# A hybrid attention block: compressed scores moved to the front, another bank for the fourth transpose, an identity made on chip, a last tile in two halves

## The chip, the cores and the metric

The kernel runs on one core of a Trainium2 chip. The metric is the device time of one execution in microseconds; the median of three runs before the change is 832.62 us (832.56 to 832.69). The core has five engines that run their own instruction streams in order and wait for each other by semaphores: PE (TensorE, matmuls and transposes), DVE (VectorE), ACT (ScalarE), POOL (GpSimd) and SP (SyncE, which here issues loads and stores). PE writes only to PSUM, which has eight banks of 512 float32 values in each of 128 partitions; all other engines' operands of this kernel lie in SBUF or in these banks.

## The reference

One decoder layer on x of 512 tokens and 1024 columns. Cut to what matters:

```python
h = rmsnorm(x, attn_norm_g)
q, k_c, v_c, k_s, v_s, k_w, v_w, nsa_gate, rwkv_in, gate_a, gate_b = split(h @ w_in)
o_a = nsa_mixer(...)        # 8 query heads of 64 in 2 groups, three branches:
   # compressed: softmax(q . kc + bias_c) vc, kc/vc = a small MLP over blocks of 32 tokens, stride 16
   # selected:   softmax over chosen blocks of 64 tokens (16 chosen, of only 8 that there are)
   # window:     softmax over the last 512 tokens
   # o = gate0 * o_cmp + gate1 * o_slc + gate2 * o_win
o_b = rwkv7_mixer(...)      # a recurrence over the tokens, 8 heads of 64
merged = sigmoid(gate_a) * (o_a @ w_proj_a) + sigmoid(gate_b) * (o_b @ w_proj_b)
x = x + merged @ w_out
u = rmsnorm(x, ffn_norm_g) @ w_up          # 1024 -> 2 * 2816
c = causal depthwise conv of width 3 over u
x = x + (silu(c_gate) * c_value) @ w_down  # 2816 -> 1024
```

Everything is float32 in and out.

## The kernel before

**Products in halves.** Large products run as three matmuls in a rounded float32 type: each operand is split into a high part (`hh`, `whi`) and a low part (`hl`, `wlo`), and hi·hi, lo·hi and hi·lo are summed in one PSUM bank. Every matmul goes through the helper `mm` (L122), every activation through `act` (L125), the additions and products of two tiles through `tt` (L128) and those by a scalar through `ts` (L132), so many rows of the profile carry these lines. Weights come through a chain of three `raw` buffers: `wload` (SP's queue) loads, ACT makes `whi`, DVE or POOL makes `wlo` (L299).

**PSUM.** Eight banks in three rotating pools: `mmb()` four, `pa()` two, `pb()` two. A pool hands its banks out in turn; the new user waits until the last reader of the old content is done. In the attention the four of `mmb()` are fixed: `Ob` collects the outputs, `db[0]` and `db[1]` alternate under dense products, `tb3` helps with transposes.

**The start.** The four token tiles of x (128 tokens each) are loaded on SP's queue, then the first weights. ACT's queue loads the 128x128 identity (`ident`, the first columns of the tile `kc`, 64 KB) and a small vector; POOL issues eight small loads of the RWKV parameters into `pra`. ACT squares each tile, DVE makes its norm and scales it, PE transposes it with `ident` (L341); PE also transposes `pra` (L356). The tile `warm`, all ones, feeds 30 matmuls that only keep PE running while x arrives.

**The attention.** There are twelve units: for the last two query tiles (qt = 3, 2) one per group g and branch b, for the first two tiles one per group with both branches in it. A unit goes through `scores`, `scale`, `turns`, `values`:

- `scores(u, n, mid)`: for each chunk, one `pa()` bank, matmuls of the queries with the keys' high and low part (KH, KL); DVE adds the bias and finds the row's extreme in one custom operation (L1171), which is the bank's only reader; ACT takes the exponential into P. After each chunk come its share of `n` fillers and the next function of the list `mid`.
- `scale(u)`: DVE and ACT multiply P by the gate over the row's sum (L1184 and after).
- `turns(u)`: PE transposes P in tiles, four 128x128 to a bank (L1204); ACT or DVE copy each bank to a slot of PTs (L1110 to L1116).
- `values(u)`: PE multiplies the transposed P with the values into `Ob`, together with the compressed branch's part (sC with `vcb`).

`compressed(qt)` makes the compressed branch for a query tile: eight 64-wide matmuls (KC) into one `pa()` bank, two reads of that bank by DVE into sC, the softmax over 32 blocks on DVE and ACT, each row scaled by its gate. It is a generator that stops once, for qt = 3, after the second read. `compressed_t(qt)` transposes sC (L1149) and ACT copies it back.

**Fillers.** The products for the gates and for `w_proj_b` are cut into single matmuls; `filler(n)` issues n of them between the other work, so that PE has something to do while DVE and ACT work on a unit. Their two banks are `db`; `nd` counts the products begun, so `db[nd[0] % 2]` is the bank that the next one will take.

**What sets the order.** In the attention PE's order is written out by hand (`tc.manual_schedule(engines=KTS)`, KTS holds PE alone); the order on DVE, ACT and POOL comes from the scheduler of the framework. The handwritten order begins: scores and scale of unit 0, `compressed(3)` to its stop, scores of unit 1, turns of unit 0, the rest of `compressed(3)`, scores of unit 2 with `compressed_t(3)` after its first chunk, values of unit 0. At the start all of PE, ACT, DVE and POOL follow the order of the code.

**The end.** The down projection runs in two halves of 512 output columns (`dense_tok`, written as the generator `dense_tok_g`). Four banks collect four token tiles over 22 row tiles of `w_down`, two per weight load; the last two loads are walked token tile by token tile, so that a finished tile is added to x1 and stored while the next one runs. For the last tile of the second half the add is done in two pieces of 256 columns, the first stored through SP's queue, the second through ACT's.

Of the kernel before, what the change touches and what calls it, by code (L numbers as in the profile page):

```python
# [16 lines left out]
ALU = mybir.AluOpType  # L17
# [6 lines left out]
NT = S // 128  # L24
KT = D // 128
# [6 lines left out]
NF = DFF // 128  # L32
# [50 lines left out]
def hybrid_block(ctx: ExitStack, tc: tile.TileContext, A: dict, out: bass.AP):  # L83
    nc = tc.nc
    v, sc, te = nc.vector, nc.scalar, nc.tensor
# [32 lines left out]
    def pb():  # L118
        return bank("b", 2)

    def mm(o, l, r, start, stop):
        te.matmul(o, lhsT=l, rhs=r, start=start, stop=stop)  # L122
# [4 lines left out]
    def tt(o, a, b, op):  # L127
        v.tensor_tensor(o, a, b, op=op)  # L128
# [12 lines left out]
    ident, mask, ones, cmask = kc[:, 0:128], kc[:, 128:256], kc[:, 256:384], kc[:, 384:416]  # L141
# [9 lines left out]
    warm = xp.tile([128, 128], F32, name="warm")  # L151
# [2 lines left out]
    pr0 = xp.tile([8, 128], F32, name="pr0")  # L154
    for t in range(NT):
        nc.sync.dma_start(xt[:, t], x_in[128 * t:128 * t + 128])
    sc.dma_start(ident, A["consts"][:, 0:128])
    sc.dma_start(pr0, A["attn_norm_g"][0].rearrange("(r p) -> r p", p=128))
    pra = xp.tile([NR0, 128], F32, name="pra")
    for name in ("rwkv_mu", "rwkv_w0", "rwkv_a0", "rwkv_k_k", "rwkv_k_a", "rwkv_r_k", "rwkv_ln_g", "rwkv_ln_b"):  # L160
        r0, n = ROWS[name]
# [170 lines left out]
    with tc.manual_schedule(engines={getattr(mybir.EngineType, e) for e in ("PE", "Activation", "DVE", "Pool")}):  # L332
# [10 lines left out]
        for t in range(NT):  # L343
            r = ssx[:, t:t + 1]
# [8 lines left out]
            if t == 1:  # L353
                pt = pts[7][:, 384:512]
# [5 lines left out]
        r0, n = ROWS["rwkv_mu"]  # L360
# [26 lines left out]
    def run(g):  # L387
        while True:
            try:
                next(g)  # L390
            except StopIteration as e:
                return e.value
# [223 lines left out]
    for g in range(2):  # L616
        for b in range(2):
            r = 64 * g + 32 * b
            v.transpose(Nn[r:r + 32].rearrange("p t s -> p t s"),
                        ABq[g][r:r + 32, :, 32 * b:32 * b + 32].rearrange("p q t -> p t q"))  # L620
    for k in range(31):
        m, n = 31 - k, k + 1
# [4 lines left out]
        stt(Tn[:, k + 1:, 0:n], tmv, 1.0, Tn[:, k + 1:, 0:n], ALU.mult, ALU.add)  # L627


    def dense_tok_g(n, xh, xl, kt=KT, halves=False):  # L630
        banks = [mmb() for _ in range(NT)]
        step = 1024 // n
        tiles = [list(range(k0, min(k0 + step, kt))) for k0 in range(0, kt, step)]

        def passes(parts, ts_):
            for part in range(2):
                for ks, w in parts:
                    for i, k in enumerate(ks):
                        for t in ts_:
                            qs = slice(128 * t, 128 * t + 128)  # L640
                            if part == 0:
                                mm(banks[t][:, 0:n], xh[:, k, qs], w[0][:, i], k == 0, False)
                                mm(banks[t][:, 0:n], xl[:, k, qs], w[0][:, i], False, False)
                            else:
                                mm(banks[t][:, 0:n], xh[:, k, qs], w[1][:, i], False, k == kt - 1)
                    if len(ts_) > 1:
                        yield

        for j, ks in enumerate(tiles[:-2]):
            parts = [(ks, wnext(len(ks), n))]  # L650
            for ts_ in ([range(2), range(2, NT)] if halves and j == 0 else [range(NT)]):
                yield from passes(parts, ts_)
        last = [(ks, wnext(len(ks), n)) for ks in tiles[-2:]]
        for t in range(NT):
            yield from passes(last, [t])
            if t < NT - 1:
                yield
        return banks

    def dense_tok(*a, **kw):  # L660
        return run(dense_tok_g(*a, **kw))
# [5 lines left out]
    vt = m2.tile([128, NT, 2, 128], F32, name="vt")  # L667
# [28 lines left out]
    pt = pa()  # L696
# [35 lines left out]
    for b in (1, 0):  # L732
        for g in range(2):
            r = 64 * g + 32 * b
# [30 lines left out]
    fill = kv_proj(1, 280)  # L765
# [159 lines left out]
    fill = fill_chain()  # L925
# [142 lines left out]
    Ob, db, tb3 = mmb(), [mmb(), mmb()], mmb()  # L1068
    nd = [0]
# [26 lines left out]
    fill = fillers()  # L1096
# [3 lines left out]
            next(fill, None)  # L1100

    oaT = m2.tile([128, 2, NH2, S], F32R, name="oaT", tag="QK")
    ev, tn = [0], [0]
    Ps, PTk = {}, {}

    PTs = hp.tile([128, 8, S], F32, name="PTs", tag="hh")
# [45 lines left out]
    def scores(u, n, mid=()):  # L1152
        qt, g, bs = u
        qs = slice(128 * qt, 128 * qt + 128)
        N = 128 * (qt + 1)
        R = 4 * len(bs)
        P = Pb[units.index(u) % 4][:, 0:R * N].rearrange("p (r n) -> p r n", n=N)
        nm = at.tile([128, 8], F32, name="nm", tag="nm", bufs=2)
        sm = at.tile([128, 8], F32, name="sm", tag="sm", bufs=2)
        per = 4 // (qt + 1)  # L1160
        nb = R // per
        for i0 in range(0, R, per):
            sp = pa()
            for i in range(i0, i0 + per):
                h, b = 4 * g + i % 4, bs[i // 4]
                o = sp[:, N * (i - i0):N * (i - i0) + N]
                mm(o, qst[:, h, qs], KH[:, b, g, 0:N], True, False)
                mm(o, qst[:, h, qs], KL[:, b, g, 0:N], False, True)
            for i in range(i0, i0 + per):
                h = 4 * g + i % 4  # L1170
                v.tensor_tensor_reduce(out=P[:, i], in0=sp[:, N * (i - i0):N * (i - i0) + N], in1=BT[:, h, 384 - 128 * qt:512],  # L1171
                                       scale=-1.0, scalar=-NEG, op0=ALU.add, op1=ALU.min, accum_out=nm[:, i:i + 1])
                act(P[:, i], P[:, i], AF.Exp, scale=-1.0, bias=nm[:, i:i + 1], accum_out=sm[:, i:i + 1])
            ib = i0 // per
            filler(n * (ib + 1) // nb - n * ib // nb)
            if ib < len(mid):
                mid[ib]()
        Ps[u] = P, sm
# [16 lines left out]
    def turns(u):  # L1195
        qt, g, bs = u
        P, _ = Ps.pop(u)
        PTk[u] = []
        for x in range(len(bs)):
            for k in range(qt + 1):  # L1200
                pt = Ob if tn[0] == 3 else tb3 if (tn[0] - (tn[0] > 3)) % 3 == 2 else pb()
                tn[0] += 1
                for i in range(4):
                    te.transpose(pt[:, 128 * i:128 * i + 128], P[:, 4 * x + i, 128 * k:128 * k + 128], ident)  # L1204
                PTk[u].append((bs[x], k, evac(pt)))

    def values(u):
        qt, g, bs = u
        qs = slice(128 * qt, 128 * qt + 128)
        O = Ob[:, 256 * g:256 * g + 256]  # L1210
        if bs[0] == 0:
            sCT = sC2[:, qt % 2].rearrange("p h n -> p (h n)")
            for j in range(2):
                for e in range(2):
                    mm(O[64 * e:64 * e + 64, 128 * j:128 * j + 128], vcb[:, 2 * g + e], sCT[:, 128 * j:128 * j + 128],
                       j == 0, False)
        for b, k, PT in PTk.pop(u):
            for r in range(2):
                mm(O[64 * r:64 * r + 64].rearrange("p (a q) -> p a q", a=2), vt[:, k, b, 64 * g:64 * g + 64],
                   PT.rearrange("p (h q) -> p h q", h=4)[:, r::2, :], False, b == 1 and k == qt)  # L1220
        if bs[-1] == 1:
            ov = O.rearrange("p (a q) -> p a q", a=2)
            act(oaT[:, 0, 2 * g:2 * g + 2, qs], ov)
            tt(oaT[:, 1, 2 * g:2 * g + 2, qs], ov, oaT[:, 0, 2 * g:2 * g + 2, qs].bitcast(F32), ALU.subtract)

    units = [(qt, g, (b,)) for qt in (3, 2) for g in range(2) for b in range(2)]
    units += [(qt, g, (0, 1)) for qt in (1, 0) for g in range(2)]
    nfill = [5, 5, 6, 6, 7, 8, 10, 10, 10, 9, 9, 6]
    with tc.manual_schedule(engines=KTS):
        after_next = (1,2,3,4,5,6,7,8,9)  # L1230
        scores(units[0], 12)
        scale(units[0])
        comp = compressed(3)
        next(comp)
        scores(units[1], 12)
        for i, u in enumerate(units):
            turns(u)
            if i == 0:
                run(comp)
            if i in (4, 8, 10):  # L1240
                compressed_t(u[0])
            if i + 2 < len(units):
                mid = [lambda: None, functools.partial(scale, units[i + 1])] if i + 1 in after_next else [lambda: None, lambda: None]
                if i == 0:
                    mid.insert(0, functools.partial(compressed_t, 3))
                scores(units[i + 2], nfill[i], mid)
                if i + 2 not in after_next:
                    scale(units[i + 2])
            else:
                filler(nfill[i])  # L1250
            if i in (1, 5, 7):
                run(compressed({1: 2, 5: 1, 7: 0}[i]))
            values(u)
        filler(100)
# [63 lines left out]
    with tc.manual_schedule(engines=KTS):  # L1318
        for t in range(NT):
            qs = slice(128 * t, 128 * t + 128)  # L1320
            p = mmb()
# [50 lines left out]
        act(aT[:, 0, f], cv)  # L1372
        tt(aT[:, 1, f], cv, aT[:, 0, f].bitcast(F32), ALU.subtract)
    for hf in range(2):
        bo = dense_tok(512, aT[:, 0], aT[:, 1], NF)
        for t in range(NT):
            n = 256 if hf and t == NT - 1 else 512
            for c0 in range(0, 512, n):
                cs = slice(512 * hf + c0, 512 * hf + c0 + n)
                tt(x1[:, t, cs], x1[:, t, cs], bo[t][:, c0:c0 + n], ALU.add)  # L1380
                (sc if c0 else nc.sync).dma_start(out[0][128 * t:128 * t + 128, cs], x1[:, t, cs])
    close(fp_cm)
    close(xr_cm)
# [26 lines left out]
```

## Time and profile before

| what | value |
| --- | --- |
| median of three runs | 832.62 us |
| the profiled execution | 832.52 us |
| its span, first to last instruction | 830.7 us |
| granted TensorE clock | 1.000 |
| PE busy | 821.3 us, 99% of the span |
| DVE, ACT, POOL busy | 514.4, 406.2, 50.7 us |
| instructions | 12893, of them 5107 matmuls |
| moved by DMA | 78.73 MB |

The page gives busy time by engine, then the span in forty slices, then the DMA queues, then the chain of work that ended last, followed back from the last instruction. The list of waits gives, for one engine, the operation that waited and whom for, with total, number and longest. In the timeline a row is start, length, engine, line, operation, output and inputs with their shapes, how many instructions the row joins, and in brackets the idle time before the first of them and what ended it. PE's matmuls are pipelined: a record ends after the next has begun, so a step is the distance of two starts. PE's name for the weight load is PEld; an engine's name with q is its DMA issue.

### The profile page before, as it was taken

What the parts mean: (1) busy time and instruction counts of PE and PEld (TensorE: products, weight loads), DVE (VectorE), ACT (ScalarE), POOL (GpSimd) and SP (SyncE); (2) the same over time, 40 slices, a digit from 0 to 9 for tenths busy, and PEclk for the clock granted to TensorE, in tenths of its full rate; (3) what the DMA queues carried; (4) which work ended last, traced back from release to release, by engine and by line L of the source; (5) the groups of instructions that cost most, each with busy time, mean ns of one, the idle gap of its engine ahead of it and who ended that gap; (6) DMA issues with size and microseconds to landing.
All of it is one profiled execution on the core that took longest, in us unless ns stands there. A gap on an engine that the chain in (4) does not pass through costs nothing.

```text
span 830.7 us, 12893 instructions
## 1 busy us (share of the span) xinstructions
PE 821.3 (99%) x5107; PEld 669.1 (81%) x5107; DVE 514.4 (62%) x1008; ACT 406.2 (49%) x793; POOL 50.7 (6%) x67
## 2 busy tenths in 40 slices
PE   8999999999999999999999999999999999999998
PEld 7777778987777887787888988888888888888886
DVE  5577789975465878787765576656665556323222
ACT  6766655454455777785334554444444444221220
POOL 6100020140000210011000000000000000000000
PEclk9999999999999999999999999999999999999999
DMA  8432222246372410001274042333333333223421
GB/s 246 107 83 63 77 77 77 71 126 185 103 128 77 90 39 19 21 26 39 78 268 136 1 119 86 100 103 102 99 89 90 101 102 103 90 89 113 140 76 51
DMA packets 109400, 78.73 MB, mean 95 GB/s; under 512 B 3877, under 2 KB 98012, under 8 KB 109340
## 3 DMA queue, kind: packets, MB, share of 16 engines
q1 hardware_dynamic: 106800, 73.92, 31.1%
q10 hardware_dynamic: 1196, 2.55, 0.9%
q0 software_dynamic: 1344, 1.45, 0.8%
q8 instruction: 40, 0.66, 0.3%
q14 instruction: 20, 0.16, 0.1%
HBM read 74.56 MB, written 2.29 MB: 93 GB/s over the span
## 4 chain that ended last, share of the span: by engine, by line
PE 95%; DVE 3%; ACT 1%; DMA 0%; issue 0%; DVEq 0%; ACTq 0%
PE ps_mm L122 84%; PE ps_a L122 5%; PE ps_b L122 2%; PE ps_b L1204 1%; PE ps_mm L1204 1%; DMA xt<-in_x_dram 0%; DVE P L1171 0%; DVE sC L128 0%; ACT P L125 0%; DVE P L132 0%; PE ps_b L536 0%; PE ps_b L567 0%; DVE PTs L1116 0%; PE ps_a L1016 0%; PE ps_b L203 0%
## 5 line engine op out<-in xcount | busy, mean ns | idle before, releaser
L299 DVE TENSOR_TENSOR wlo<-raw,whi 128x1024 fp32r<-128x1024 f32 (+1 forms) x111 | 131.5, 1185 | 184.5 <-PE ps_mm L122 160.0
L122 PE MATMUL ps_mm<-hh,whi 128*128 128x512 f32 (+1 forms) x624 | 242.7, 391 | 0.5 <-DVE hl L137 0.5
L122 PE MATMUL ps_mm<-hl,whi 128*128 128x512 f32 (+1 forms) x624 | 240.5, 388 | 0.0
L125 ACT ACTIVATE whi<-raw 128x1024 fp32r<-128x1024 f32 (+3 forms) x124 | 123.3, 996 | 158.6 <-PE ps_mm L122 143.2
L122 PE MATMUL ps_mm<-hh,wlo 128*128 128x512 f32 (+1 forms) x624 | 152.1, 384 | 0.0
L122 PEld LDWEIGHTS ps_mm<-hh,whi 128*128 128x128 f32 x624 | 117.3, 188 | 27.2 <-issue 1.0
L122 PEld LDWEIGHTS ps_mm<-hl,whi 128*128 128x128 f32 x624 | 117.5, 188 | 22.9 <-issue 1.0
L122 PEld LDWEIGHTS ps_mm<-hh,wlo 128*128 128x128 f32 x624 | 115.2, 188 | 23.4
L122 PE MATMUL ps_mm<-whi,aT 128*128 128x512 f32 x352 | 84.5, 390 | 0.0
L122 PEld LDWEIGHTS ps_mm<-whi,aT 128*128 128x128 f32 x352 | 66.0, 188 | 14.3 <-issue 0.4
L137 DVE SCALAR_TENSOR_TENSOR cgv<-ps_mm,cw,cgv 128x511 f32<-128x511 f32 (+1 forms) x88 | 65.4, 746 | 1.6
L125 ACT ACTIVATE cgv<-ps_mm,cw 128x512 f32<-128x512 f32 x44 | 34.2, 780 | 23.3 <-PE ps_mm L122 23.3
L122 PE MATMUL ps_mm<-wlo,aT 128*128 128x512 f32 x176 | 44.3, 390 | 0.0
L125 ACT ACTIVATE aT<-cgv 128x512 fp32r<-128x512 f32 x22 | 13.9, 632 | 56.8 <-DVE cgv L128 56.8
L125 ACT ACTIVATE P<-P,nm 128x512 f32<-128x512 f32 (+3 forms) x64 | 35.4, 554 | 12.2 <-DVE nm L1171 12.0
L122 PEld LDWEIGHTS ps_mm<-wlo,aT 128*128 128x128 f32 x176 | 33.1, 188 | 6.9
L125 ACT ACTIVATE cgv<-cgv 128x512 f32<-128x512 f32 x22 | 13.9, 632 | 41.0 <-DVE cgv L137 41.0
L299 POOL TENSOR_TENSOR wlo<-raw,whi 128x512 fp32r<-128x512 f32 (+3 forms) x13 | 21.1, 1620 | 200.9 <-PE ps_mm L122 132.2
L1171 DVE CUSTOM_DVE_ANT_0 P<-ps_a,AB 128x512 f32<-128x512 f32 (+3 forms) x64 | 29.3, 486 | 4.1 <-PE ps_a L122 3.9
L128 DVE TENSOR_TENSOR x<-x,ps_mm 128x512 f32<-128x512 f32 (+1 forms) x17 | 11.0, 655 | 23.2 <-PE ps_mm L122 21.3
L128 DVE TENSOR_TENSOR aT<-cgv,aT 128x512 fp32r<-128x512 f32 x22 | 15.2, 693 | 14.7 <-ACT aT L125 14.7
L125 ACT ACTIVATE QK<-ps_mm 128x64 f32<-128x64 f32 (+5 forms) x56 | 14.8, 308 | 17.5 <-PE ps_mm L122 17.4
(357 smaller groups left out, 1206.0 us busy)
## 6 DMA issues: line engine op xcount, KB each, us to landing
raw<-in_w_up_dram SPq DMA_DIRECT2D x44, 512.0 KB, 3.8
raw<-in_w_in_dram SPq DMA_DIRECT2D x38, 512.0 KB, 3.9
raw<-in_w_down_dram SPq DMA_DIRECT2D x22, 512.0 KB, 3.6
raw<-in_w_out_dram SPq DMA_DIRECT2D x8, 512.0 KB, 4.0
xt<-in_x_dram SPq DMA_DIRECT2D x4, 512.0 KB, 4.1
raw<-in_cmp_w_v_dram SPq DMA_DIRECT2D x4, 512.0 KB, 3.8
raw<-in_w_proj_b_dram SPq DMA_DIRECT2D x8, 256.0 KB, 2.8
raw<-in_w_proj_a_dram SPq DMA_DIRECT2D x8, 256.0 KB, 2.7
```

Source lines behind the costliest of these rows:

```text
L122: te.matmul(o, lhsT=l, rhs=r, start=start, stop=stop)
L125: sc.activation(o, i, f, **kw)
L128: v.tensor_tensor(o, a, b, op=op)
L137: v.scalar_tensor_tensor(o, a, s, b, op0=op0, op1=op1)
L299: low = eng.tensor_tensor(lo, raw, hi.bitcast(F32), op=ALU.subtract)
L1171: v.tensor_tensor_reduce(out=P[:, i], in0=sp[:, N * (i - i0):N * (i - i0) + N], in1=BT[:, h, 384 - 128 * qt:512], scale=-1.0, scalar=-NEG, ...
L1204: te.transpose(pt[:, 128 * i:128 * i + 128], P[:, 4 * x + i, 128 * k:128 * k + 128], ident)
```

## The change

Five edits.

1. The identity is no longer loaded. POOL makes it by a selection on `warm` (ones where row and column number agree, zero elsewhere), placed behind the first of the eight `pra` loads in POOL's stream, where the instruction that configures POOL now stands too; the other seven loads follow it. ACT's queue loses one DMA.
2. The last token tile of the down projection's second half: the twelve 512-wide matmuls of its last two weight loads become 24 of 256. First all for columns 0 to 255 into the old bank, then all for columns 256 to 511 into a new bank of `pb()`. Columns 256 to 511 so end in two partial sums, and DVE adds both to x1, one 256-wide add more than before.
3. `compressed(3)` is run whole before the scores of unit 0; `compressed_t(3)` stands after the second score chunk of unit 2 in place of the first.
4. In `turns` the bank of a tile follows its place in the unit: two of `pb()`, then `tb3`, and a fourth tile takes `Ob` (unit 0) or the filler bank `db[nd[0] % 2]`. Before, one counter over all units rotated over `pb()`, `pb()`, `tb3`, with `Ob` once.
5. In `values` the products with PTs come first and open the accumulation; the compressed part comes last and closes it.

```diff
-    sc.dma_start(ident, A["consts"][:, 0:128])
+    nc.gpsimd.affine_select(ident, warm, pattern=[[-1, 128]], compare_op=ALU.is_equal, fill=0.0, base=0,
+                            channel_multiplier=1)
...
+        def split_end(parts):
+            qs = slice(128 * NT - 128, 128 * NT)
+            banks.append(pb())
+            for c0, o in ((0, banks[NT - 1][:, 0:256]), (256, banks[NT][:, 0:256])):
+                cs = slice(c0, c0 + 256)
+                for part in range(2):
+                    for ks, w in parts:
+                        for i, k in enumerate(ks):
+                            mm(o, xh[:, k, qs], w[part][:, i, cs], c0 > 0 and part == 0 and k == parts[0][0][0],
+                               part == 1 and k == kt - 1)
+                            if part == 0:
+                                mm(o, xl[:, k, qs], w[0][:, i, cs], False, False)
...
-            yield from passes(last, [t])
+            if ends and t == NT - 1:
+                split_end(last)
+            else:
+                yield from passes(last, [t])
...
-                pt = Ob if tn[0] == 3 else tb3 if (tn[0] - (tn[0] > 3)) % 3 == 2 else pb()
-                tn[0] += 1
+                j = len(PTk[u])
+                pt = pb() if j < 2 else tb3 if j == 2 else Ob if u == units[0] else db[nd[0] % 2]
...
+        PT = PTk.pop(u)
+        for b, k, T in PT:
+            for r in range(2):
+                mm(O[64 * r:64 * r + 64].rearrange("p (a q) -> p a q", a=2), vt[:, k, b, 64 * g:64 * g + 64],
+                   T.rearrange("p (h q) -> p h q", h=4)[:, r::2, :], b == 0 and k == 0, b == 1 and k == qt and len(bs) == 1)
         if bs[0] == 0:
...
-                       j == 0, False)
...
+                       False, j == 1 and len(bs) == 2)
...
+        run(compressed(3))
         scores(units[0], 12)
         scale(units[0])
-        comp = compressed(3)
-        next(comp)
         scores(units[1], 12)
         for i, u in enumerate(units):
             turns(u)
-            if i == 0:
-                run(comp)
...
-                    mid.insert(0, functools.partial(compressed_t, 3))
+                    mid.insert(1, functools.partial(compressed_t, 3))
...
-        bo = dense_tok(512, aT[:, 0], aT[:, 1], NF)
+        bo = dense_tok(512, aT[:, 0], aT[:, 1], NF, ends=hf == 1)
...
+                if c0:
+                    tt(x1[:, t, cs], x1[:, t, cs], bo[NT][:, 0:n], ALU.add)
```

More of the change, by code (lines that the diff above doesn't have):

```diff
@@ L627, in hybrid_block, with dense_tok_g @@
         stt(Tn[:, k + 1:, 0:n], tmv, 1.0, Tn[:, k + 1:, 0:n], ALU.mult, ALU.add)
-    def dense_tok_g(n, xh, xl, kt=KT, halves=False):
+    def dense_tok_g(n, xh, xl, kt=KT, halves=False, ends=False):
         banks = [mmb() for _ in range(NT)]
@@ L1102, in hybrid_block @@
     oaT = m2.tile([128, 2, NH2, S], F32R, name="oaT", tag="QK")
-    ev, tn = [0], [0]
+    ev = [0]
     Ps, PTk = {}, {}
@@ L1215, in values @@
                     mm(O[64 * e:64 * e + 64, 128 * j:128 * j + 128], vcb[:, 2 * g + e], sCT[:, 128 * j:128 * j + 128],
-                       j == 0, False)
[L1217 to L1220, printed above, removed]
+                       False, j == 1 and len(bs) == 2)
         if bs[-1] == 1:
```

## The prediction

> **What bounds the kernel now.** I read the page's busy shares first, then its chain, then the list of PE's waits, then the timeline where a wait is listed.
>
> ```profile
> span 830.7 us, 12893 instructions
> ...
> PE 821.3 (99%) x5107; PEld 669.1 (81%) x5107; DVE 514.4 (62%) x1008; ACT 406.2 (49%) x793; POOL 50.7 (6%) x67
> ...
> GB/s 246 107 83 63 77 77 77 71 126 185 103 128 77 90 39 19 21 26 39 78 268 136 1 119 86 100 103 102 99 89 90 101 102 103 90 89 113 140 76 51
> ...
> PE 95%; DVE 3%; ACT 1%; DMA 0%; issue 0%; DVEq 0%; ACTq 0%
> ```
> ```profile
> PE ps_mm L1204 <- ACT PTs L125: 0.6, 1, 0.6
> PE ps_mm L122 <- DVE hl L137: 0.5, 1, 0.5
> ```
>
> PE is busy in 99% of the span and makes 95% of the chain, and no edit takes a matmul away. All that can be won is idle time of PE: at the start, in the attention, and behind its last matmul. The waits listed are small because a record runs on past the start of the next one; stalls have to be read from start to start. First, what one step of PE costs:
>
> ```profile
> 823.96 1.98 PE L122 MATMUL ps_mm<-whi,aT 128*128 128x512 f32 x8
> 825.77 1.07 PE L122 MATMUL ps_mm<-wlo,aT 128*128 128x512 f32 x4
> ```
> ```profile
> 464.62 0.28 PE L122 MATMUL ps_mm<-hh,whi 128*128 128x256 f32 x1
> 464.74 0.28 PE L122 MATMUL ps_mm<-hl,whi 128*128 128x256 f32 x1
> ```
>
> Four more 512-wide matmuls take 1.98 − 1.07 = 0.91 us, 0.227 each (a last record is then 1.07 − 3 × 0.227 = 0.39 long). A 256-wide one steps by 0.12.
>
> **Compressed scores first.** PE's starts in the attention's first scores:
>
> ```profile
> 298.94 0.39 PE L122 MATMUL ps_a<-KH,qst 128*128 128x512 f32 x1
> ...
> 303.55 0.98 PE L122 MATMUL ps_a<-KC,qst 128*128 128x64 f32 x8
> ...
> 305.37 0.40 PE L122 MATMUL ps_mm<-hh,whi 128*128 128x512 f32 x1
> 305.87 0.50 PE L122 MATMUL ps_a<-KH,qst 128*128 128x512 f32 x1
> 306.20 0.39 PE L122 MATMUL ps_a<-KL,qst 128*128 128x512 f32 x1
> ...
> 306.66 0.62 PE L122 MATMUL ps_mm<-hh,wlo 128*128 128x512 f32 x2
> 307.48 0.47 PE L122 MATMUL ps_a<-KH,qst 128*128 128x512 f32 x1 [0.19 <-DVE sC L128]
> ...
> 312.09 0.40 PE L122 MATMUL ps_mm<-obT,whi 128*128 128x512 f32 x1
> 312.95 0.41 PE L1149 MATMUL ps_mm<-kc,sC 128*128 128x128 f32 x2 [0.46 <-DVE sm L128]
> ```
>
> Start to start less 0.227 (twice that for the pair at 306.66): 0.27 before 305.87, 0.37 before 307.48, 0.63 before 312.95. After a stall the next step is 0.1 longer (305.87 to 306.20 is 0.33), so these three are worth 1.27 + 0.3 = 1.57 us. The cause is banks. The compressed scores (KC) take one of the two a-banks at 303.55, after the first unit, and keep it until DVE has read it twice; meanwhile two chunks of the second unit follow each other in the other bank. DVE's rows:
>
> ```profile
> 300.29 0.88 DVE L128 TENSOR_TENSOR obT<-BO,obT 128x512 fp32r<-128x512 f32 x1
> ...
> 304.74 0.39 DVE L128 TENSOR_TENSOR sC<-ps_a,BC 128x256 f32<-128x256 f32 x1
> ...
> 306.92 0.41 DVE L128 TENSOR_TENSOR sC<-sC,ps_a 128x256 f32<-128x256 f32 x1
> ...
> 312.38 0.43 DVE L128 TENSOR_TENSOR sC<-sC,mx 128x256 f32<-128x256 f32 x1
> ```
>
> Between the two reads DVE does other work until 306.92, and the softmax ends at 312.81, which the transposes at 312.95 wait for. In the changed order KC stands at 298.94, and the eight end some 0.9 later at 299.84. The first read runs from about 299.95 to 300.3, then DVE's order has the add into obT (to 301.1, the next start being 0.8 after 300.29), then the second read to 301.5. The first unit's chunk 0 takes the other bank; chunk 1 needs KC's. It would be due one chunk (five steps, 1.14) after 299.84, at 300.98, and starts at 301.55: **a new stall** of 0.57, with its restart 0.67. Behind it the two banks alternate strictly, so the stalls before 305.87 and 307.48 go, and the softmax starts nearly five us earlier and is over before the compressed transposes, which also stand one score chunk later. Walking DVE and ACT on through the new order with these lengths, the third unit's first chunks come 0.1 later than now, behind the second unit's scaling, and the backlog that makes this one stall is gone:
>
> ```profile
> 321.21 0.40 PE L122 MATMUL ps_mm<-obT,whi 128*128 128x512 f32 x1
> 321.60 0.50 PE L122 MATMUL ps_a<-KH,qst 128*128 128x512 f32 x1
> ```
>
> That is 0.39 − 0.227 + 0.1 = 0.26. Sum: −1.57 + 0.67 + 0.1 − 0.26, about **−1.1 us**. Bounds: −1.4, if the 0.1 doesn't come and the add into obT takes 0.2 less; +0.3, if the softmax, now among the first unit's reads on DVE, holds these up by operations of some 0.4 and the stalls only move.
>
> **The banks of the transposes.** Before, the tiles of all units rotate over three banks, so a unit's fourth tile asks for a bank just used. Now it takes one of the two filler banks. The two places where this costs:
>
> ```profile
> 333.82 1.04 PE L1204 MATMUL ps_b<-kc,P 128*128 128x128 f32 x8
> ...
> 335.45 0.66 PE L1204 MATMUL ps_mm<-kc,P 128*128 128x128 f32 x4 [0.59 <-ACT PTs L125]
> ```
> ```profile
> 371.47 0.60 PE L1204 MATMUL ps_mm<-kc,P 128*128 128x128 f32 x4
> 372.28 0.66 PE L1204 MATMUL ps_b<-kc,P 128*128 128x128 f32 x4 [0.21 <-ACT PTs L125]
> ```
>
> Eight transposes take 1.04 and four 0.60, so one steps by 0.11. At the first place the next is due 8 × 0.11 after 333.82, at 334.70, and starts 0.75 late; at the second 371.91 is due and 372.28 comes, 0.37. Both go if a filler bank is free there, and the one taken is the one to be filled next, so empty. What is late next:
>
> ```profile
> 336.21 0.69 DVE L1116 COPY PTs<-ps_mm 128x512 f32<-128x512 f32 x1 [0.30 <-PE ps_mm L1204]
> 336.82 0.55 DVE L1171 CUSTOM_DVE_ANT_0 P<-ps_a,AB 128x384 f32<-128x384 f32 x1
> ```
>
> DVE copies the fourth tile and only then reads the scores whose bank the next unit's third chunk waits for. PE comes 0.75 earlier, DVE some 0.4 (its 0.30 of waiting and a little overlap), so 0.35 comes back as a wait there: net 0.40. At the second place the copy of the filler bank runs from about 372.6 to 373.3; that bank's next filler stands behind four pairs of scores, past 374. **−0.77 us** in all; bounds 0 (fillers wait for the copies as long as the transposes did) and −1.12.
>
> **Values before compressed.** The same matmuls in another order: 0. Four compressed matmuls, 0.44 by the transposes' step, covered the last tile's evacuation; left as cover are a unit's fillers, five or more of 0.227, so 1.14, against a copy of 0.69. Without that cover 0.25 (0.69 − 0.44) would show, once or twice: bounds 0 and +0.5.
>
> **The identity made by GpSimd.** The rows of the start:
>
> ```profile
> 4.96 0.51 POOL L165 DMA_DIRECT2D pra<-in_rwkv_ln_b_dram  x1
> 5.45 0.29 POOL L919 MEMSET BC<- 128x200 f32 x1
> ...
> 10.36 0.26 PE L356 MATMUL ps_b<-kc,pra 42*128 42x42 f32 x1
> ...
> 11.86 2.51 POOL L363 TENSOR_TENSOR wlo<-raw,whi 128x512 fp32r<-128x512 f32 x2 [6.11 <-ACT whi L125]
> 12.01 2.42 ACT L125 ACTIVATE hh<-ps_mm,ang 128x512 fp32r<-128x512 f32 x4 [0.24 <-PE ps_mm L341]
> ```
> ```profile
> kc<-in_consts_dram ACTq DMA_DIRECT2D x1, 64.0 KB, 4.2
> ...
> pra<-in_rwkv_ln_b_dram POOLq DMA_DIRECT2D x1, 2.0 KB, 5.0
> ```
>
> A transfer of 64 KB leaves the time in which x arrives; at the first slice's 246 GB/s it is 0.27 us. The selection goes to POOL behind the first of the eight small pra loads, ahead of seven. Its length no row shows: 0.29 by the MEMSET of 128x200, 1.25 by one TENSOR_TENSOR of 128x512. I take 0.6, nearer to the MEMSET: it handles 128 columns, but reads and compares. The seven issues move by that; the last load landed at 4.96 + 5.0 = 9.96 and is used at 10.36, and ACT stood idle for 0.24 more before hh. So 0.64 is free, and 1.25 would cost 0.6. The identity itself is there before 4, no later than the load's 4.2 us. PE's first waits end with x and its norms; I count about half of what x can gain, **−0.1 us**, bounds −0.27 and +0.6. [...]
>
> **The halved last tile.** Twelve steps of 0.227 (2.72) become 24 of 0.12 (2.88): PE ends 0.16 later, less 0.11 for the shorter last record (0.28 for 0.39).
>
> ```profile
> 826.88 0.75 DVE L128 TENSOR_TENSOR x<-x,ps_mm 128x256 f32<-128x256 f32 x2 [2.03 <-PE ps_mm L122]
> 827.66 0.38 ACTq L1381 DMA_DIRECT2D out_dram<-x  x1
> ```
>
> Two adds of 0.375 stood behind PE. The first half's add and store and the second half's first add now run beside the last twelve matmuls (1.44 us), since these write another bank; one add stays. 0.16 − 0.375 is about **−0.2 us**; bounds −0.33, and +0.5 if all three adds wait for the end. The last store's 3 us to the end of the span stay.
>
> **The sum.** −1.1 − 0.77 − 0.1 − 0.2 = −2.2 us against the profiled execution's 832.52, so 830.3; the runs' median, 832.62, lies 0.1 above, and I say 830.4. All lower bounds together give −3.1, all upper ones +1.9. What a measurement can tell from no change here is about 0.2%, 1.67 us.
>
> **The rivals.** First: not the banks but DVE sets the pace of the attention's start. For it: the new stall is made by DVE's own add of 0.88. Then the first scores gain 0.2, the transposes 0.4, start and tail 0.3: −0.9, 831.7, nothing that can be told. Against: both stalls of the second unit come from a bank that is freed early in the new order.
>
> Second, the slower side: the selection is late. It is the first computation that POOL does after its configuration is set, and both now stand ahead of seven loads, where before idle time of 6.11 us lay behind. It decides from 0.64 us on. The whole 6.11 with 0.6 would move the last pra issue to 11.67 and its landing to 16.67, 6.3 past its use, less 0.24: +6.1, with the other gains 836.6. Against: the first two TENSOR_TENSORs after that idle time take 2.51 together, so neither shows a late start, and the MEMSET 0.29. [...]
>
> Third: the waits that I let return don't: −1.4 − 1.12 − 0.27 − 0.33 = −3.1, 829.5.
>
> **How the numbers follow.** My sum, within 0.5 us, 0.45; no returning waits 0.12; DVE's pace 0.32; the selection late by more than its slack 0.11. Faster by over 0.2% holds the first two but a little of their lower end: 0.54; slower by over 0.2% the late selection, if by several us: 0.10; the rest, 0.36, lies within. From 829.4 to 832.6 the range holds all but the slower case and some of DVE's.
>
> **What the new profile would show.** Right: KC ahead of the first KH; a gap of about half a microsecond before the second score chunk, put down to sC, none before the second unit's; the compressed transposes without a wait; a fourth tile's transposes 0.11 behind the third's and a short wait two score chunks later; 256-wide matmuls at the end and one add behind them; a selection of 0.3 to 1.3 us on POOL at about 2. Wrong: PE's first transposes waiting for POOL, or the one of pra for its load; fillers waiting for a copy of PTs; DVE's two reads of KC's bank as far apart as before.

## The result and the profile after

The changed kernel takes 830.63 us in the median (830.48 to 830.97), against 832.60 of the kernel before beside it: ratio 0.9976, 95% interval 0.9969 to 0.9984, so 1.97 us less. The forecast was 830.4.

The page of the changed kernel, the same lines as before:

```profile
span 828.9 us, 12923 instructions
...
PE 821.7 (99%) x5119; PEld 671.5 (81%) x5119; DVE 515.4 (62%) x1009; ACT 405.3 (49%) x793; POOL 50.3 (6%) x68
...
PE 95%; DVE 3%; ACT 1%; DMA 0%; issue 0%; DVEq 0%; ACTq 0%
```

The span is 1.8 us shorter, PE has twelve matmuls more and is the bound as before. From its list of waits:

```profile
PE ps_mm L122 <- DVE hl L137: 0.5, 1, 0.5
PE ps_a L122 <- DVE sC L128: 0.5, 1, 0.5
PE ps_a L122 <- DVE nm L1189: 0.3, 1, 0.3
```

The waits for PTs and the one of the transposes for `sm` are off the list; a longer one for sC and one for `nm` are new. PE's timeline of the attention's first scores (start, length, operation, idle time before it):

```profile
298.80 0.98 PE L122 MATMUL ps_a<-KC,qst 128*128 128x64 f32 x8
...
300.62 0.40 PE L122 MATMUL ps_mm<-hh,whi 128*128 128x512 f32 x1
301.51 0.47 PE L122 MATMUL ps_a<-KH,qst 128*128 128x512 f32 x1 [0.49 <-DVE sC L128]
...
306.00 0.40 PE L122 MATMUL ps_mm<-hh,whi 128*128 128x512 f32 x1
306.23 0.40 PE L122 MATMUL ps_a<-KH,qst 128*128 128x512 f32 x1
...
312.63 0.39 PE L122 MATMUL ps_mm<-obT,whi 128*128 128x512 f32 x1
312.86 0.38 PE L1167 MATMUL ps_mm<-kc,sC 128*128 128x128 f32 x2
313.34 0.50 PE L122 MATMUL ps_a<-KH,qst 128*128 128x512 f32 x1
```

KC stands first, and the second chunk starts 0.89 behind the filler at 300.62, so waits 0.66. The second unit's chunk at 306.23 follows in 0.23, without a wait, and the compressed transposes at 312.86 too. The chunk behind the transposes comes 0.26 late (0.48 less two steps of 0.11). DVE there:

```profile
299.81 0.43 DVE L128 TENSOR_TENSOR sC<-ps_a,BC 128x256 f32<-128x256 f32 x1 [0.80 <-PE ps_a L122]
300.16 0.87 DVE L128 TENSOR_TENSOR obT<-BO,obT 128x512 fp32r<-128x512 f32 x1
300.95 0.41 DVE L128 TENSOR_TENSOR sC<-sC,ps_a 128x256 f32<-128x256 f32 x1
301.28 0.68 DVE L1189 CUSTOM_DVE_ANT_0 P<-ps_a,AB 128x512 f32<-128x512 f32 x1
```

The two reads of KC's bank are 1.1 us apart with the add into obT between them. The place of the fourth unit's transposes, in PE's timeline:

```profile
333.48 1.04 PE L1223 MATMUL ps_mm<-kc,P 128*128 128x128 f32 x8
...
335.29 0.63 PE L122 MATMUL ps_mm<-obT,whi 128*128 128x512 f32 x2
336.25 0.44 PE L122 MATMUL ps_a<-KH,qst 128*128 128x384 f32 x1 [0.33 <-DVE nm L1189]
```

Third and fourth tile run as eight transposes without a gap. At 336.25 PE waits 0.5; in the kernel before 0.1 of that stood at the same place already (336.88 to 337.44 for two steps). The last rows of the kernel, PE's, DVE's and ACT's queue:

```profile
824.72 0.64 PE L122 MATMUL ps_b<-wlo,aT 128*128 128x256 f32 x4
```
```profile
825.39 0.42 DVE L128 TENSOR_TENSOR x<-x,ps_b 128x256 f32<-128x256 f32 x1 [0.68 <-PE ps_b L122]
825.85 0.38 ACTq L1400 DMA_DIRECT2D out_dram<-x  x1
```

One add stands behind PE. Taking starts from the two timelines, the span divides like this (us; the rows are PE's, "third chunk" the KH of a unit's third score chunk):

| stretch | before | after | difference |
| --- | --- | --- | --- |
| to the first dense matmul | 13.54 | 13.43 | −0.11 |
| to the attention's first score matmul | 298.94 | 298.80 | −0.14 |
| from there to the fourth unit's third chunk | 22.66 | 22.03 | −0.63 |
| on to the sixth unit's third chunk | 15.84 | 15.42 | −0.42 |
| on to the last transposes | 55.74 | 55.31 | −0.43 |
| first matmul of the last tile to the end | 6.74 | 6.56 | −0.18 |

The stretches between agree within 0.05. 0.14 + 0.63 + 0.85 + 0.18 is the 1.8 of the spans. The two starts are one execution each; how far such a start moves from one execution to the next is shown below.

### The profile page after: what moved, and what is told of

Same layout as the page of the kernel before. It is cut to its first block, busy times and chain, and to the rows that moved or that the text cites. A ratio compares the mean times of both kernels' runs of the same rounds, so it can differ in the third digit from the quotient of the medians.

```text
span 828.9 us, 12923 instructions
## 1 busy us (share of the span) xinstructions
PE 821.7 (99%) x5119; PEld 671.5 (81%) x5119; DVE 515.4 (62%) x1009; ACT 405.3 (49%) x793; POOL 50.3 (6%) x68
## 4 chain that ended last, share of the span: by engine, by line
PE 95%; DVE 3%; ACT 1%; DMA 0%; issue 0%; DVEq 0%; ACTq 0%
PE ps_mm L122 84%; PE ps_a L122 5%; PE ps_b L122 2%; PE ps_b L1223 1%; PE ps_mm L1223 1%; DMA xt<-in_x_dram 0%; DVE PTs L1134 0%; DVE P L132 0%; DVE sC L128 0%; DVE P L1189 0%; PE ps_b L537 0%; PE ps_b L568 0%; PE ps_a L1034 0%; PE ps_a L204 0%; PE ps_b L204 0%; PE ps_a L898 0%
## 5 line engine op out<-in xcount | busy, mean ns | idle before, releaser
L122 PE MATMUL ps_mm<-whi,aT 128*128 128x512 f32 (+1 forms) x352 | 83.6, 387 | 0.0
L122 PE MATMUL ps_mm<-wlo,aT 128*128 128x512 f32 (+1 forms) x176 | 43.9, 387 | 0.0
```

## The experiments

**Each edit alone.** The third, on the kernel before:

```diff
+        run(compressed(3))
         scores(units[0], 12)
         scale(units[0])
-        comp = compressed(3)
-        next(comp)
...
-                    mid.insert(0, functools.partial(compressed_t, 3))
+                    mid.insert(1, functools.partial(compressed_t, 3))
```

> The kernel before with the third edit alone: compressed scores whole before the first unit, the compressed transposes one score chunk later. Banks theory (mine): the compressed scores' bank is freed early, so the waits before the second unit's second and third chunk (0.27 and 0.37 us) and before the compressed transposes (0.63) go, and one new wait of 0.66 stands before the first unit's second chunk. From the two traces, read at the fourth unit's second chunk, the first scores gained about 0.65 us, less than the 1.1 of the prediction; so 832.6 - 0.65 = 831.95. DVE theory (rival): DVE's own work sets the pace, the waits only move to later chunks: within 0.2 us of the kernel before.

Measured: 832.16 (832.01 to 832.33) against 832.63; ratio 0.9994, interval 0.9986 to 1.0003. In the trace the stretch to the fourth unit's third chunk is 22.17, 0.49 less than before. The interval holds 1, but the slowest of these eleven executions, 832.33, lies below the fastest of the kernel before, 832.41. The gain is there, and it is less than half of the 1.1 of the prediction and below the 0.65 expected here.

The same, with the compressed transposes left in their old place (`mid.insert(0, ...)`):

> As the run with the third edit alone, but the compressed transposes stay where they were, after the first score chunk of the third unit. If the early softmax alone takes away their wait, the time is that of the run with the third edit, within 0.1 us. If the place counts too, they now wait for ACT's copy out of the bank that they share with the transposes of the first unit (that copy ends some 0.3 us after they are due), and the time is 0.2 to 0.4 us above that run.

Measured: 832.22 (832.09 to 832.65), ratio 0.9995 (0.9986 to 1.0004); the medians alone don't tell the two apart. The traces do: the stretch is 22.34, 0.17 longer, and the wait has changed its owner.

```profile
312.17 0.40 PE L122 MATMUL ps_mm<-obT,whi 128*128 128x512 f32 x1
312.75 0.44 PE L1149 MATMUL ps_mm<-kc,sC 128*128 128x128 f32 x2 [0.19 <-ACT PTs L125]
```

The transposes start 0.58 behind the filler, 0.35 late, and wait for ACT's copy out of the bank, not for the softmax. So both halves of the edit count, by these traces: the early softmax, and the later place.

The fourth edit alone:

```diff
-                pt = Ob if tn[0] == 3 else tb3 if (tn[0] - (tn[0] > 3)) % 3 == 2 else pb()
-                tn[0] += 1
+                j = len(PTk[u])
+                pt = pb() if j < 2 else tb3 if j == 2 else Ob if u == units[0] else db[nd[0] % 2]
```

> The kernel before with the fourth edit alone: the fourth tile of transposes takes a filler bank. My theory: the gaps of 0.75 and 0.37 us go, and about 0.35 us comes back before the sixth unit's third score chunk: 832.6 - 0.8 = 831.8. Rival: the fillers wait for the copies in place of the transposes: 832.6, with waits of fillers for PTs copies in the trace.

Measured: 831.77 (831.51 to 832.05) against 832.63; ratio 0.9990, interval 0.9981 to 0.9998. From the first score matmul to the last transposes its trace has 93.36 us where the kernel before has 94.24: −0.88. No filler waits for a copy. This edit does nearly half of the whole change; the forecast gave it a third (0.77 of 2.2). Over the same stretch the third edit alone has 93.78, so −0.46, and the changed kernel 92.76, so −1.48: the two together give 0.14 more than one by one.

The fifth edit alone, the order in `values`:

```diff
+        PT = PTk.pop(u)
+        for b, k, T in PT:
...
         if bs[0] == 0:
...
-        for b, k, PT in PTk.pop(u):
...
```

> The kernel before with the fifth edit alone: the products with the transposed P first, the compressed part last. My theory: no wait was covered by the compressed part, so 832.6 within 0.1 us. Rival: the last copy of a unit is late, and one or two waits of 0.25 us appear: 832.9 to 833.1.

Measured: 832.67 (832.43 to 833.08), ratio 1.0000 (0.9991 to 1.0009); the same stretch in the trace is 94.23 against 94.24. It does nothing that can be told here.

The second edit alone (the halved last tile, as in the diff of the change):

> The kernel before with the second edit alone: the last token tile's last products in halves of 256 columns. My theory: PE ends 0.05 to 0.16 us later, one add of 0.4 stands behind it in place of two: 832.6 - 0.2 = 832.4. Rival: the adds wait for the very last matmul all the same: 833.1.

Measured: 832.38 (832.21 to 832.61) against 832.55, ratio 0.9998 (0.9988 to 1.0007); by the executions alone that isn't told from no change. From the last tile's first matmul to the end the trace has 6.52 for 6.74.

The first edit alone:

```diff
-    sc.dma_start(ident, A["consts"][:, 0:128])
+    nc.gpsimd.affine_select(ident, warm, pattern=[[-1, 128]], compare_op=ALU.is_equal, fill=0.0, base=0,
+                            channel_multiplier=1)
```

> The kernel before with the first edit alone: the identity made by GpSimd. My theory: 0.1 to 0.15 us less before the first dense matmul, nothing elsewhere: 832.5. The selection took 0.32 us in the changed kernel, so a late start of GpSimd (rival, 6 us) isn't expected any more.

Measured: 832.72 (832.24 to 833.31) against 832.55 (832.39 to 832.86); ratio 1.0001, interval 0.9992 to 1.0010. No gain, and twice the spread. The traced execution is the slowest of the eleven, 833.31; ACT's timeline (the first row) and PE's (the second) show what was bad in it:

```profile
8.06 1.06 ACT L125 ACTIVATE h<-xt 128x1024 f32<-128x1024 f32 x1 [0.84 <-DMA xt<-in_x_dram]
```
```profile
10.74 0.23 PE L357 MATMUL ps_b<-kc,pra 42*128 42x42 f32 x1 [0.78 <-DMA pra<-in_rwkv_ln_b_dram]
```

The third tile of x comes late (ACT waits 0.84 for it; in the kernel before it squares that tile at 7.59 without a wait), and then PE waits 0.78 for the last small load; the first dense matmul starts at 14.31 in place of 13.54. In the kernels that load the identity it starts at 13.54 to 13.76, in all eight of their traces.

**What the delay of the small loads costs.** The changed kernel, the selection five times over:

```diff
-    nc.gpsimd.affine_select(ident, warm, ...)
+    for _ in range(5):
+        nc.gpsimd.affine_select(ident, warm, ...)
```

> The changed kernel with the selection made five times over in place of once: four more of 0.32 us ahead of the seven small loads. If the slack that I gave that queue is right in its kind, the loads land 1.0 to 1.3 us later, about 0.1 of that is free at the transposes of the parameters and some 0.2 more on ACT, and the time is 0.7 to 1.0 us above the changed kernel: 831.3 to 831.6. If the loads are not on the path, 830.6.

Measured: 832.45 (831.43 to 833.15). The four more selections of 0.31 put the last issue at 6.48, and PE's timeline has

```profile
11.65 0.23 PE L358 MATMUL ps_b<-kc,pra 42*128 42x42 f32 x1 [1.48 <-DMA pra<-in_rwkv_ln_b_dram]
```

so the loads are on the path at once: the first dense matmul is at 14.52, 1.1 behind the changed kernel's 13.43. Five of the eleven executions took 831.43 to 832.07, one of them within the 831.3 to 831.6 expected and four above it, and six 832.45 or more; what these have in common is told in the last section.

**The bank or DVE?** The compressed scores of the last query tile in `Ob`, which is free until the transposes:

```diff
-        pc = pa().rearrange("p (j g e a n) -> p j g e a n", j=2, g=2, e=2, a=2)
+        pc = (Ob if qt == NT - 1 else pa()).rearrange("p (j g e a n) -> p j g e a n", j=2, g=2, e=2, a=2)
```

> The changed kernel with the compressed scores of the last query tile in the bank that collects the outputs, which nobody needs before the transposes, in place of one of the two score banks. Banks theory: the new wait of 0.66 us (with its restart 0.74) before the first unit's second chunk goes and nothing takes its place: 830.6 - 0.7 = 829.9. DVE theory: DVE still has the same operations in the same order before the first unit's scores are read, so the wait moves to the third chunk and the next ones and less than 0.3 us is gained: 830.4 or more.

Measured: 831.45 (830.65 to 832.61), with a disturbed start that hides the answer; inside the attention the trace gives it. The second chunk comes 2.05 after the first matmul in place of 2.71, so the wait of 0.66 is gone. But the stretch to the fourth unit's third chunk is 22.11, no shorter than 22.03. The wait stands elsewhere now, in front of the second unit's fourth chunk (PE, then DVE):

```profile
309.15 0.86 PE L122 MATMUL ps_mm<-hh,wlo 128*128 128x512 f32 x3
310.44 0.50 PE L122 MATMUL ps_a<-KH,qst 128*128 128x512 f32 x1 [0.43 <-DVE nm L1189]
```
```profile
308.90 0.88 DVE L132 TENSOR_SCALAR P<-P,sm 128x512 f32<-128x512 f32 x2
309.70 0.68 DVE L1189 CUSTOM_DVE_ANT_0 P<-ps_a,AB 128x512 f32<-128x512 f32 x1
```

Three steps behind 309.15 the chunk was due at 309.83; it starts at 310.44, when DVE, busy with the scaling of the first unit, has read the bank. Over the whole attention, from its first matmul to the last transposes, this kernel has 92.83 and the changed one 92.76. A freed bank alone only moves the wait here, as the first rival said. Why DVE is late at the new place is the order that the scheduler gave it. In the changed kernel DVE reads the second unit's second chunk first and scales the first unit after that:

```profile
306.97 0.68 DVE L1189 CUSTOM_DVE_ANT_0 P<-ps_a,AB 128x512 f32<-128x512 f32 x1
307.57 1.27 DVE L132 TENSOR_SCALAR P<-P,sm 128x512 f32<-128x512 f32 x3
```

With the compressed scores in their own bank the scaling stands ahead of that read (the rows at 308.90 and 309.70). DVE has little room either way: from its first read of KC to its last read of the second unit's scores it is busy for 9.91 of 10.26 us in the changed kernel and for 9.71 of 10.17 here. Whether another order on DVE would have kept the gain of the bank was not tested.

**Less work on DVE, and the identity loaded.** Three kernels side by side: the changed kernel again, the changed kernel with the first edit undone, and this last one with three copies given to ACT:

```diff
-        if ev[0] % 2 == 0 or ev[0] in (3,27):
+        if ev[0] % 2 == 0 or ev[0] in (3,7,11,15,27):
             act(PT, pt)
```

> The changed kernel once more, beside the two that follow, on the same chip. On the chip of the runs with the first edit alone and with the other bank, the small loads on GpSimd's queue and the tiles of x came late and executions differed by over a microsecond. If that goes with the chip or the occasion, the changed kernel is now at 830.9 to 831.6 with a spread of about 1 us; if it goes with those kernels, it is at 830.6 again with a spread of 0.5.

> The changed kernel with its first edit undone: the identity is loaded by ACT's queue as before, the other four edits stay. From the runs of the single edits: 832.55 - 0.46 (third) - 0.88 (fourth) - 0.15 (second), less 0.1 where the third and fourth help each other: 831.0, with a spread of about 0.5 us. If making the identity on chip is a gain of 0.1 as I forecast, this is 0.1 above the changed kernel of the same call; if it costs where the loads come late, this is 0.2 to 0.8 below it.

> The changed kernel with the identity loaded, and in addition the copies of the fourth tile of transposes of the second, third and fourth unit made by ACT in place of DVE. If DVE is the pace where stalls came back (its copy stands ahead of its reads of the scores), the waits before the third score chunks of the fourth, fifth and sixth unit (0.28, 0.19, 0.60 in the changed kernel's trace) go: 0.8 to 1.1 below the kernel with the identity loaded. If ACT is the pace as much as DVE, its exponentials come later and less than 0.3 is gained.

Measured, beside 832.71 (832.47 to 833.07) of the kernel before:

| kernel | median (range) us | ratio, 95% interval |
| --- | --- | --- |
| changed kernel again | 830.86 (830.35 to 831.49) | 0.9978, 0.9969 to 0.9987 |
| identity loaded | 830.90 (830.71 to 831.17) | 0.9978, 0.9969 to 0.9987 |
| identity loaded, copies on ACT | 829.96 (829.80 to 830.25) | 0.9967, 0.9954 to 0.9979 |

Here the first edit gains nothing, and the range is 1.14 us with it and 0.46 without. In the first measurement of the changed kernel it was 0.49, so the wide range is not there every time. The new trace of the changed kernel holds one of the prediction's signs of being wrong, a wait of the parameters' transpose for its load:

```profile
10.32 0.23 PE L357 MATMUL ps_b<-kc,pra 42*128 42x42 f32 x1 [0.29 <-DMA pra<-in_rwkv_ln_b_dram]
```

Its first dense matmul is still at 13.61, and at 13.72 where the identity is loaded. The copies give 0.94 more, and the largest of the waits that had come back is gone; PE's timeline of the last kernel at the place of the 0.5:

```profile
335.23 0.63 PE L122 MATMUL ps_mm<-obT,whi 128*128 128x512 f32 x2
335.69 0.34 PE L122 MATMUL ps_a<-KH,qst 128*128 128x384 f32 x1
```

0.46 is two steps of 0.23: no wait. Up to the fourth unit's third chunk its trace has 21.88 for 22.03, up to the sixth unit's 36.60 for 37.45. The slowest execution of this kernel, 830.25, lies below the fastest of the other two, 830.35. What the copies did in the first of these stretches can be read at the fourth unit's third chunk. In the changed kernel DVE copies the second unit's fourth tile just before it reads the scores whose bank that chunk needs; PE starts the chunk at 320.83, when the read is over:

```profile
319.48 0.69 DVE L1134 COPY PTs<-ps_mm 128x512 f32<-128x512 f32 x1 [0.18 <-PE ps_mm L1223]
320.09 0.68 DVE L1189 CUSTOM_DVE_ANT_0 P<-ps_a,AB 128x512 f32<-128x512 f32 x1
```

With that copy on ACT the same chunk follows its filler in one step and 0.03 (PE):

```profile
320.72 0.40 PE L122 MATMUL ps_mm<-obT,whi 128*128 128x512 f32 x1
320.98 0.50 PE L122 MATMUL ps_a<-KH,qst 128*128 128x512 f32 x1
```

**The selection behind the small loads.** The kernel with the copies on ACT, the identity made by GpSimd again, but after all eight loads:

```diff
-    sc.dma_start(ident, A["consts"][:, 0:128])
...
         nc.gpsimd.dma_start(pra[r0:r0 + n], src[0].rearrange("(r p) -> r p", p=128))
+    nc.gpsimd.affine_select(ident, warm, pattern=[[-1, 128]], compare_op=ALU.is_equal, fill=0.0, base=0,
+                            channel_multiplier=1)
```

> The kernel with the fourth tiles copied by ACT (829.96), but with the identity made by GpSimd again, now behind all eight small loads in place of behind the first. If the delay of the seven loads is what takes the gain of the missing 64 KB and spreads the times, PE has no wait for these loads, and the time is 829.4 to 829.9 with a spread of 0.5. If the late tiles of x, beside weight loads that now start earlier, do it, the spread stays at about 1 us and the time at 829.9 to 830.4.

Measured: 830.18 (829.52 to 830.46) against 832.70; ratio 0.9969, interval 0.9957 to 0.9981. The loads are issued about as early as before (the last at 5.01, before at 4.96), and PE still waits for the last one:

```profile
10.36 0.23 PE L357 MATMUL ps_b<-kc,pra 42*128 42x42 f32 x1 [0.26 <-DMA pra<-in_rwkv_ln_b_dram]
```

and x's third tile is late again (ACT waits 0.49 for it). So the delay in the queue is not the whole of it: in this trace, without the 64 KB load, the other loads land at other times (the last small one 5.2 after its issue, before 5.0), and x's first tile comes earlier (squares at 4.51, before at 4.84) while its third comes later (7.84, before 7.59). What orders them was not settled.

## Why the prediction was right

The time and the direction were right, and each of the four terms went the forecast way in the trace on record. Their order was not right: the first term was too large by nearly half a microsecond, so that the banks, forecast second, gave the most. By the spans the sum of −2.2 came out as −1.8.

- **The banks of the transposes**, −0.77 forecast, −0.85 in the trace and −0.88 alone: right by its own steps. Both gaps went. What came back at 336.25 was 0.4 for a forecast 0.35 (0.5 by start to start, less the 0.1 that had stood there), so the first place gave 0.42 for 0.40; the second gave 0.43 for 0.37.
- **Compressed scores first**, −1.1 forecast, −0.63 measured, −0.49 alone. The mechanism was right up to the new stall, and the 0.1 for the third unit's chunk came as booked (0.26 in place of 0.17). Three sizes were off, by 0.47 together. The largest: "the backlog that makes this one stall is gone" was wrong. The fourth unit's third chunk waits as before (the change leaves 320.43 to 320.83, 0.40, where 0.39 was), so 0.26 was not gained; what holds it is DVE's copy ahead of its read, for with this copy on ACT the wait is 0.03. Second, the wait of the compressed transposes was booked at 0.73 with its restart and was worth 0.58: in the kernel before, the score chunk behind the transposes starts at 313.12, 1.03 behind the filler at 312.09; less 0.227 and two steps of 0.11 that is 0.58, so there is no restart. Third, the new stall was 0.66 with a restart of 0.07, where 0.57 and 0.1 were booked. DVE's three operations up to there were forecast to 0.01 (the second read ends at 301.36), but PE starts 0.15 behind the end of that read, as it starts 0.14 behind the softmax in the kernel before (312.81 to 312.95); the forecast had 0.05. The rows of the kernel before for the second size:

```profile
312.95 0.41 PE L1149 MATMUL ps_mm<-kc,sC 128*128 128x128 f32 x2 [0.46 <-DVE sm L128]
313.12 0.48 PE L122 MATMUL ps_a<-KH,qst 128*128 128x512 f32 x1
```

- **Banks or DVE.** The first rival, which was given 0.32, was wrong in its time, 831.7, and right in part of its mechanism. In the prediction the two were alternatives; the runs show two limits close to each other. The banks are shown by the third and fourth edit alone. DVE is shown by the bank that brought nothing (22.11 against 22.03) and by the three copies, which brought 0.15 in that stretch and 0.94 in all, most of it where waits had come back behind the fourth edit.
- **The halved last tile**, −0.2 forecast, −0.18 in the trace, −0.17 alone.
- **Values before compressed**, 0 forecast, 0.04 alone, within what can be told. The cover that the prediction puts at 0.44 is 0.48 in the trace (315.89 to 316.37, eight records); nothing hangs on it.
- **The identity**, −0.1 forecast, −0.11 in the trace on record. As a mean this is not borne out: by the medians it is 0.04 less than the kernel that loads the identity beside it, and 0.17 more than the kernel before when it is the only edit; by single traces it goes from −0.1 to +0.8. That the first trace shows the forecast size is therefore one sample and partly luck. The step that failed is the count of slack: 0.64 us between landing and use, taken from one execution, is not there when the loads land later (PE waited 0.29, 0.78 and 0.99 for the last one in three traces with the selection behind the first load). With four selections more the path grew by 1.1 where 0.7 to 1.0 was expected.
- **The late selection**, the slower rival, did not happen:

```profile
1.34 0.67 POOL L166 DMA_DIRECT2D pra<-in_rwkv_mu_dram  x1 [0.83 <-POOLq L1416]
2.10 0.32 POOL L157 TENSOR_SCALAR_AFFINE_SELECT kc<-warm 128x128 f32<-128x128 f32 x1
2.35 0.57 POOL L166 DMA_DIRECT2D pra<-in_rwkv_w_dram  x1
```

The selection starts at 2.10, 0.09 behind the end of the first load's issue (1.34 + 0.67), and takes 0.32, close to the lower bound; the next issue follows at 2.35. So the 6.11 us that this rival moved the loads by are not in the trace: the last of them is issued at 5.38, 0.42 later than the 4.96 of the kernel before.

## What to carry to other kernels

A gap of PE in front of a bank had two owners in these kernels, the bank and the engine that reads it, and before a gain is booked the reader's own order has to be walked to the end of the stretch. Here a freed bank moved a wait without shortening the stretch, and giving some of the reader's work to another engine was worth more (0.15 in that stretch, 0.94 in all). And slack at a kernel's start that hangs on the landing of loads should be read from several executions; one of them is a sample: in its two traces the changed kernel had no wait for the last small load, and one of 0.29.

## What the chip showed beside that

PE's clock is not the same in every execution of the start. From 7 to 25 us it was granted in full (1.00) in the traces of the changed kernel, of the first edit alone and of the five selections. In the run with the compressed scores in their own bank, two stretches of the trace, with their length, PE's busy time (and matmuls), its granted clock, the summed share of the DMA engines and GB/s:

```profile
9.00:13.40 4.40, 3.07 (x23) 0.97 1.17 299
13.40:16.50 3.10, 3.10 (x10) 0.50 0.46 141
```

In this execution PE had waited 0.99 us for the small loads; from 9.0 to 13.4 it was busy for 3.07 of 4.40, with transposes. The granted clock is 1.00 from 12 to 13, 0.57 from 13 to 14, 0.50 from 14 to 16, 0.72 from 16 to 17 and 1.00 from 17 to 25. If it only goes between full and half, an estimate from these means, it falls at about 13.14, 1.2 us before the first dense matmul at 14.31, and is back at about 16.55, 3.4 us later. Between the first dense matmul and the attention the trace has 286.40 us where the changed kernel has 285.37, so 1.03 more. The mean clock of this execution is 0.998. In the kernel with five selections the mean clock tells the executions apart: six with 0.998 took 832.45 to 833.15, five with 1.0 took 831.43 to 832.07. So a wait of a microsecond at the start went with a loss of nearly two here (0.88 at the first dense matmul and 1.03 behind it), but need not: the traced execution with five selections waited 1.48 and the one with the first edit alone 0.78, both at the full clock. That the wait brought the half clock on is my guess; no run shows what did.
